# Attention stage of a hybrid layer: group norms shared out to ScalarE and GpSimd, the queries' turn at another place in the pair, the score maximum accumulated

## The chip, the cores and the metric

One core of one Trainium2 chip runs the kernel. The metric is the time of one execution on the device in microseconds, and the median of several runs counts. The core has five engines with a queue each, which they work off in order: TensorE (PE in the profile, PEld for its weight loads), VectorE (DVE), ScalarE (ACT), GpSimd (POOL) and SyncE (SP, which issues the transfers here).

## The reference, cut to what matters

One layer over 1024 latent tokens and 256 context tokens, width 1024, in float32. Half of the width goes through a convolution module, half through attention with 8 query heads on 2 key heads of 64 elements. Only the attention's part matters here:

```
u = rms_norm(x, norm_w) * (1.0 + scale) + shift
p = u @ w_in
q, k, v = qk_heads(p, q_norm_w, k_norm_w)      # each head of q and k divided by its root mean square, times a weight
q = rope_2d(q, angles)                         # x1*cos - x2*sin, x1*sin + x2*cos, by row and by column of the grid
k = rope_2d(k, angles)
k_all, v_all = concat([k_ctx, k]), concat([v_ctx, v])          # 1280 keys
s = einsum('bqkgd,bskd->bkgqs', q, k_all) / sqrt(64)
pr = softmax(s, axis=-1)
attn = einsum('bkgqs,bskd->bqkgd', pr, v_all) * silu(p[..., ZA_LO:ZA_HI])
out = concat([attn, conv]) @ w_out
h = x + gate * out
```

## The kernel before, in words

Products that need more precision than one pass gives are made from a high and a low part: "hi" is a copy rounded by the engine that writes it, "lo" the difference that is left. The kernel has four stages: the modulation and the turned tokens (`start`), the projections with the convolution taps (`project`), the attention, and the rest of the convolution module with the output projection.

The queries are made in two halves c (heads 0 to 3 and 4 to 7) and four groups g of 256 tokens. `norm_rope` (L540) takes the projected 128x512 block of a half and group from PSUM. ACT squares it, DVE sums the squares per head, DVE scales the sum and POOL raises it to the power -1/2 (`rstd`, L118). DVE multiplies the block by a cosine and by a sine table (L561, tiles q11t and the like), POOL adds the crossed halves (L567) and multiplies by the root (L568, tile q11o). `q_split` (L597) makes hi on ACT and lo on DVE, tile hl. `q_turn` (L602) turns half of a block, two heads, with four transposes on PE into a PSUM bank (qt), and ACT copies that to qT. All groups of half 0 and group 0 of half 1 are done in `project`. Groups 1 to 3 of half 1 are projected, normed, split and turned by hooks within the attention.

The attention works on pairs of heads: a unit u is one group and one head, a pair is two units, and there are 16 pairs. Within a pair each of two units has two blocks of 128 queries. For every unit and block t the steps are qa and qb (scores against 1280 keys, the part in banks of its own and the part in the shared bank of the score tile s), ma and mb (the negative maximum of each part, DVE), mc (the smaller of the two), ex (exponential on ACT with its sum, which needs the final maximum). Then for five parts k of the keys tr (four transposes of the exponentials into a PSUM bank pt), ra (raw copy out of the bank by ACT, for three of the five), hi (ACT or DVE), lo (DVE where hi is ACT's, else POOL), pv (the product with v). After that come the sum's reciprocal rz, the gate gs on POOL, ol and ad (the sum of the high and low halves), and once a pair gt, mu, mh, ml. A step is named by its kind, unit and number: lo14 is the lo part of unit 1, part 4.

What sets the order is the table ORDER: a planned time in the pair for each step, with a period of 13.4 (PERIOD) between pairs. Steps and hooks are issued in the order of these times, on each engine's queue, and the engines keep that order. The hooks have planned times of their own: QP for the two projections of a group, QN for its norm, QS for its split, QT for the turn within each of the first 14 pairs. A tile of a pool may be used again once its last reader has been issued; the engine that writes it next then waits for that reader. PSUM has two banks of tag t in this stage, which tr, gt, the turn and the projection of group 2 share. Groups 1 and 3 are projected into the bank of tag acc, which pv uses too.

The score tile s is laid out so that both blocks share one bank for 256 keys each: the part qb of one block can be written only when the exponential of the other has read the bank. This is why qb waits for an ex.

In pairs 8 to 15 another hook splits a piece of the later weights on DVE (wo0h, wo0l and so on). Behind the attention the order is left to a scheduler.

Of the kernel before, what the change touches and what calls it, by code (L numbers as in the profile page):

```python
# [11 lines left out]
BF16 = mybir.dt.bfloat16  # L12
AF = mybir.ActivationFunctionType
ALU = mybir.AluOpType
AX = mybir.AxisListType
# [3 lines left out]
P = 128  # L19
# [4 lines left out]
DH = 64  # L24
KEYS = S + CTX
# [5 lines left out]


ORDER = {
# [17 lines left out]
QP = (-2.0, -1.99), (3.9, 3.91), (7.09, 7.19)  # L51
QN = 1.32, 7.57, 8.5
QS = 6.0, 11.0, 13.45
QT = 4.0

TAP, AHEAD = 1.33, 3.0
NPT = 0, 5, 5, 5
# [23 lines left out]
class Layer:  # L81
# [455 lines left out]
        self.mc[g] = hi, lo  # L537


    def norm_rope(self, ps, nh, g, table, name):  # L540

        nc = self.nc
        n = 2 * nh
        w = n * DH
        pv = ps.rearrange("p t (h d) -> p t h d", d=DH)
        sq = self.w2([P, 2, nh, DH], f"{name}sq")
        nc.scalar.activation(sq, pv, AF.Square)
        ss = self.small([P, 16], "qss", "qss")[:, 0:n]
        nc.vector.tensor_reduce(out=ss, in_=sq.rearrange("p t h d -> p (t h) d"), axis=AX.X, op=ALU.add)
        r = self.small([P, 16], "qr", "qr")[:, 0:n]  # L550
        self.rstd(r, ss, 1.0 / DH)
        out = self.w2([P, n, DH], f"{name}o")
        if table is None:
            for t in range(2):
                nc.vector.tensor_mul(out=out[:, t * nh:(t + 1) * nh], in0=pv[:, t],
                                     in1=self.wkn.unsqueeze(1).broadcast_to([P, nh, DH]))
        else:
            t1 = self.w2([P, 2, nh, DH], f"{name}t1")
            t2 = self.w2([P, 2, nh, DH], f"{name}t2")
            for i, t in enumerate((t1, t2)):  # L560
                nc.vector.tensor_mul(out=t, in0=pv, in1=table[:, i, 2 * g:2 * g + 2, :].unsqueeze(2)  # L561
                                     .broadcast_to([P, 2, nh, DH]))
            ov, v1, v2 = (x.rearrange(s, s=2, e=16) for x, s in (
                (out, "p h (x s e) -> p s (h x) e"), (t1, "p t h (x s e) -> p s (t h x) e"),
                (t2, "p t h (x s e) -> p s (t h x) e")))
            for s in range(2):
                nc.gpsimd.tensor_add(out=ov[:, s], in0=v1[:, s], in1=v2[:, 1 - s])  # L567
        nc.gpsimd.tensor_mul(out=out, in0=out, in1=r.unsqueeze(2).broadcast_to([P, n, DH]))  # L568
        return out
# [22 lines left out]

    def q(self, c, g, ps):

        return self.norm_rope(ps, 4, g, self.tq, f"q{c}{g}")

    def q_split(self, c, g, x):  # L597
        hl = self.b4([P, 8, 2, DH], f"hl{c}{g}", F32R)
        self.split(hl[:, :, 0], hl[:, :, 1], x)
        return hl  # L600

    def q_turn(self, c, g, hl, hp):  # L602
# [47 lines left out]

    def op_ma(self, u, t):
        st = self.st[u]
        st["nm", t] = nm = self.small([P, 3], "nm", "nm")
        r = self.nc.vector.reduce_max(out=nm[:, 0:1], in_=self.s5[:, 1536 * t:1536 * t + 1024], axis=AX.X, negate=True)  # L654
        self.s_deps("DVE", r, [st["q", t, 0]])

    def op_mb(self, u, t):
        st = self.st[u]
        r = self.nc.vector.reduce_max(out=st["nm", t][:, 1:2], in_=self.s5[:, 1024 + 256 * t:1280 + 256 * t],  # L659
                                      axis=AX.X, negate=True)  # L660
        self.s_deps("DVE", r, [st["q", t, 1]])

    def op_mc(self, u, t):
        nm = self.st[u]["nm", t]
        self.nc.vector.tensor_tensor(out=nm[:, 2:3], in0=nm[:, 0:1], in1=nm[:, 1:2], op=ALU.min)  # L665

    def op_ex(self, u, t):
        nc, st = self.nc, self.st[u]
        if "z" not in st:
            st["z"] = self.small([P, 2], "z", "z")  # L670
        st["e", t] = e = self.e5.tile([P, KEYS], F32, tag="e", name=f"e{u[0]}{u[1]}{t}")
        ex = nc.scalar.activation(e, self.s5[:, t * KEYS:(t + 1) * KEYS], AF.Exp, bias=st["nm", t][:, 2:3],  # L672
                                  accum_out=st["z"][:, t:t + 1])
        self.s_deps("ACT", ex, [st["q", t, 0], st["q", t, 1]])
        self.s_use[t] = ex.ins

    def op_tr(self, u, k):
# [392 lines left out]
```

## Time and profile before

| What | Value |
|---|---|
| Median of 3 runs | 684.87 us (683.95 to 687.38) |
| The profiled execution | 683.55 us, span 681.7 us |
| PE busy | 650.2 us (95%) |
| DVE busy | 537.4 us (79%) |
| ACT busy | 352.9 us (52%) |
| POOL busy | 332.5 us (49%) |

The span is what the engines' records cover; the execution's own time lies 1.85 us above it. The attention goes from the first scores at 298.5 us to about 550 us. A share of busy time over the whole span mixes stages with different limits, so the rows are read by stage. Rows of the timeline give start, length, engine, line, operation and tiles of instructions that follow each other, how many there are, and in brackets the idle time in front and the instruction that ended it.

### The profile page before, as it was taken

How to read it: one execution, taken by the hardware profiler on the slowest of the kernel's cores; microseconds unless marked ns; L12 is line 12 of the kernel's file. 1: busy time of each engine (PE TensorE's matmuls, PEld its weight loads, DVE VectorE, ACT ScalarE, POOL GpSimd, SP SyncE). 2: the span in 40 equal slices, each digit the busy share in tenths (PEclk: the TensorE clock that was granted, in tenths of full speed). 3: DMA queues.
4: the chain of work that ended last, by engine and by line, in shares of the span. 5: the costliest groups of instructions: out<-in, count | busy, mean ns of one | idle time of the engine just before them, and what ended most of it. 6: DMA issues, size and time to landing. Idle time of an engine off the chain costs nothing.

```text
span 681.7 us, 11003 instructions
## 1 busy us (share of the span) xinstructions
PE 650.2 (95%) x4258; PEld 572.3 (84%) x4258; DVE 537.4 (79%) x844; ACT 352.9 (52%) x578; POOL 332.5 (49%) x289
## 2 busy tenths in 40 slices
PE   4989999999999999997999999899999999999997
PEld 1467799888888999996899999888888878888885
DVE  2698789749999999876999999999999953545422
ACT  3564325554343122226888888788888845441000
POOL 1244804957329132885656766565566564121200
PEclk9899999999999999999999999999999999999999
DMA  8984310312653232100010001000100021133711
GB/s 266 319 225 129 116 36 1 94 31 62 217 185 124 71 101 78 32 1 1 1 32 1 1 32 60 3 32 25 40 1 1 1 93 32 62 124 132 256 60 46
DMA packets 51251, 53.28 MB, mean 78 GB/s; under 512 B 4521, under 2 KB 41697, under 8 KB 51200
## 3 DMA queue, kind: packets, MB, share of 16 engines
q1 hardware_dynamic: 51104, 52.57, 24.4%
q8 instruction: 33, 0.54, 0.3%
q14 instruction: 18, 0.15, 0.1%
q10 hardware_dynamic: 96, 0.02, 0.0%
HBM read 44.20 MB, written 8.39 MB: 77 GB/s over the span
## 4 chain that ended last, share of the span: by engine, by line
PE 67%; DVE 23%; issue 3%; DMA 3%; ACT 2%; SPq 1%; POOL 0%; DVEq 0%; ACTq 0%
PE o L820 12%; PE pv L715 8%; PE s L636 8%; PE pt L682 7%; DVE y L456 6%; PE g L386 6%; PE a L386 6%; PE kv L412 4%; DVE yp L456 4%; PE pw L531 3%; PE zc L386 3%; PE q L412 3%; DVE p L700 3%; DVE nm L654 2%; DMA wm<-in_w_mod 2%
## 5 line engine op out<-in xcount | busy, mean ns | idle before, releaser
L706 POOL TENSOR_TENSOR p<-raw,p 128x512 fp32r<-128x512 f32 x96 | 127.0, 1337 | 81.2 <-DVE p L700 70.8
L636 PE MATMUL s<-kT,qT 128*128 128x512 f32 (+1 forms) x384 | 100.8, 372 | 4.6 <-ACT e L672 4.5
L715 PE MATMUL pv<-p,v 128*128 128x256 f32 x640 | 103.2, 292 | 0.7 <-DVE mm L747 0.7
L456 DVE SCALAR_TENSOR_TENSOR yp<-up,cw,yp 128x1024 f32<-128x1024 f32 x77 | 99.1, 1287 | 1.9
L682 PE MATMUL pt<-ident,e 128*128 128x128 f32 x640 | 93.5, 273 | 1.0 <-DVE p L706 0.8
L672 ACT ACTIVATE e<-s,nm 128x1280 f32<-128x1280 f32 x64 | 85.0, 1329 | 14.3 <-DVE nm L665 14.1
L715 PEld LDWEIGHTS pv<-p,v 128*128 128x128 f32 x640 | 85.9, 189 | 4.5 <-DVE mm L747 1.5
L654 DVE TENSOR_REDUCE nm<-s 128x1 f32<-128x1024 f32 x64 | 77.7, 1214 | 0.6
L682 PEld LDWEIGHTS pt<-ident,e 128*128 128x128 f32 x640 | 73.3, 141 | 2.6 <-PE pv L715 1.2
L636 PEld LDWEIGHTS s<-kT,qT 128*128 128x128 f32 x384 | 62.7, 189 | 11.6 <-ACT e L672 5.7
L691 ACT ACTIVATE raw<-pt 128x512 f32<-128x512 f32 x96 | 57.5, 600 | 9.6 <-PE pt L682 5.5
L700 DVE CAST p<-raw 128x512 fp32r<-128x512 f32 x96 | 47.3, 520 | 1.8 <-ACT raw L691 1.2
L698 ACT ACTIVATE p<-pt 128x512 fp32r<-128x512 f32 x64 | 38.5, 602 | 11.6 <-PE pt L682 10.3
L706 DVE TENSOR_TENSOR p<-pt,p 128x512 fp32r<-128x512 f32 x64 | 40.9, 676 | 1.4 <-ACT p L698 1.4
L456 DVE SCALAR_TENSOR_TENSOR y<-up,cw,y 128x1024 f32<-128x1024 f32 x25 | 40.8, 1632 | 0.8
L833 DVE TENSOR_TENSOR r<-o,gb 128x512 f32<-128x512 f32 (+1 forms) x17 | 10.8, 656 | 30.6 <-PE o L820 30.6
L659 DVE TENSOR_REDUCE nm<-s 128x1 f32<-128x256 f32 x64 | 26.9, 421 | 9.1 <-PE s L636 7.7
L441 POOL TENSOR_TENSOR yz<-yz,ct 128x512 f32<-128x512 f32 x24 | 33.6, 1433 | 0.0
L123 POOL TENSOR_TENSOR qr<-qr,mhalf 128x8 f32<-128x8 f32 (+1 forms) x13 | 21.5, 1657 | 9.0 <-DVE qr L122 8.8
L440 ACT ACTIVATE ct<-up,cw 128x512 f32<-128x512 f32 x24 | 15.7, 713 | 12.9 <-DVE up L424 9.9
L116 POOL TENSOR_TENSOR ul<-u,uh 128x512 fp32r<-128x512 f32 x8 | 12.2, 1528 | 20.2 <-DVE uh L114 13.6
L665 DVE TENSOR_TENSOR nm<-nm 128x1 f32<-128x1 f32 x64 | 20.2, 315 | 1.7
(578 smaller groups left out, 1751.7 us busy)
## 6 DMA issues: line engine op xcount, KB each, us to landing
x<-in_x SPq DMA_DIRECT2D x8, 512.0 KB, 5.5
wg<-in_w_mod SPq DMA_DIRECT2D x8, 512.0 KB, 4.0
xr<-in_x SPq DMA_DIRECT2D x8, 512.0 KB, 8.7
out<-r SPq DMA_DIRECT2D x15, 256.0 KB, 2.0
wm<-in_w_mod SPq DMA_DIRECT2D x12, 256.0 KB, 6.7
zc_d<-zc SPq DMA_DIRECT2D x4, 512.0 KB, 3.3
za_d<-za SPq DMA_DIRECT2D x4, 512.0 KB, 4.1
zar<-za_d SPq DMA_DIRECT2D x4, 512.0 KB
```

Source lines behind the costliest of these rows:

```text
L386: nc.tensor.matmul(acc[h], lhsT=ww, rhs=uu[k][:, h * 512:(h + 1) * 512], start=first and i == 0, stop=last and i == 2)
L412: self.nc.tensor.matmul(acc[:, t * 256:(t + 1) * 256], lhsT=x, rhs=y, start=k == 0 and i == 0, stop=k == NK - 1 and i == 2)
L456: nc.vector.scalar_tensor_tensor(out=out, in0=up[:, w:w + S], scalar=cw[:, w:w + 1], in1=y if w else st["y2"], op0=ALU.mult, op1=ALU.add)
L636: mm = nc.tensor.matmul(self.s5[:, s0 + k0:s0 + k0 + n], lhsT=qt[:, h % 4, t * P:(t + 1) * P], rhs=kT[:, w, k0:k0 + n], start=w == 0, stop ...
L654: r = self.nc.vector.reduce_max(out=nm[:, 0:1], in_=self.s5[:, 1536 * t:1536 * t + 1024], axis=AX.X, negate=True)
L672: ex = nc.scalar.activation(e, self.s5[:, t * KEYS:(t + 1) * KEYS], AF.Exp, bias=st["nm", t][:, 2:3], accum_out=st["z"][:, t:t + 1])
L682: nc.tensor.transpose(out=tp[:, i * 256 + t * P:i * 256 + (t + 1) * P], in_=st["e", t][:, (2 * k + i) * P:(2 * k + i + 1) * P], identity=s ...
L691: self.nc.scalar.activation(raw, st["T", k], AF.Copy)
L700: nc.vector.tensor_copy(out=st["p", k][:, 0], in_=st["T", k])
L706: eng.tensor_sub(out=p[:, 1], in0=st["T", k], in1=p[:, 0].bitcast(F32))
L715: nc.tensor.matmul(st["pv"][:, 0:256], lhsT=self.v[:, kt, u[1] // 4].rearrange("p w d -> p (w d)"), rhs=st["p", k][:, j, i * 256:(i + 1) * ...
L820: self.nc.tensor.matmul(o, lhsT=p, rhs=q, start=half == k == i == 0, stop=half == 1 and k == 3 and i == 2)
```

## The change

It does three things.

- The norm of groups 1 to 3 of half 1 gets a copy of the projected block from PSUM to SBUF by ACT (tile q11c and the like), the two products with the tables go from DVE to POOL, and so does the lo part of the split.
- The planned time of the queries' turn goes from 4.0 to 7.4.
- The maximum of the second part of the scores becomes one operation that multiplies by -1, takes the smaller with the first part's result as a per-row scalar, and accumulates the minimum; the separate step mc is gone, and ex reads the accumulated value. A junk tile takes the elementwise output.

```
-    "qa00": 0.0, "qb00": 1.04, "ma00": 2.04, "mb00": 2.2, "mc00": 2.74, "ex00": 3.76, "qa01": 3.85, "qb01": 4.53,
+    "qa00": 0.0, "qb00": 1.04, "ma00": 2.04, "mb00": 2.2, "ex00": 3.76, "qa01": 3.85, "qb01": 4.53,
...
 QP = (-2.0, -1.99), (3.9, 3.91), (7.09, 7.19)
 QN = 1.32, 7.57, 8.5
 QS = 6.0, 11.0, 13.45
-QT = 4.0
+QT = 7.4
...
-    def norm_rope(self, ps, nh, g, table, name):
+    def norm_rope(self, ps, nh, g, table, name, pool=False):
...
         out = self.w2([P, n, DH], f"{name}o")
+        eng = nc.vector
+        if pool:
+            eng, pc = nc.gpsimd, self.w2([P, 2, nh, DH], f"{name}c")
+            nc.scalar.activation(pc, pv, AF.Copy)
+            pv = pc
...
             for i, t in enumerate((t1, t2)):
-                nc.vector.tensor_mul(out=t, in0=pv, in1=table[:, i, 2 * g:2 * g + 2, :].unsqueeze(2)
+                eng.tensor_mul(out=t, in0=pv, in1=table[:, i, 2 * g:2 * g + 2, :].unsqueeze(2)
                                      .broadcast_to([P, 2, nh, DH]))
...
-        return self.norm_rope(ps, 4, g, self.tq, f"q{c}{g}")
+        return self.norm_rope(ps, 4, g, self.tq, f"q{c}{g}", pool=c == 1 and g > 0)
...
-        self.split(hl[:, :, 0], hl[:, :, 1], x)
+        self.split(hl[:, :, 0], hl[:, :, 1], x, lo_on="pool" if c == 1 and g else "dve")
...
     def op_mb(self, u, t):
         st = self.st[u]
-        r = self.nc.vector.reduce_max(out=st["nm", t][:, 1:2], in_=self.s5[:, 1024 + 256 * t:1280 + 256 * t],
-                                      axis=AX.X, negate=True)
+        nm = st["nm", t]
+        junk = self.sm.tile([P, 256], BF16, tag="mj", name="mj", bufs=2)
+        r = self.nc.vector.tensor_scalar(out=junk, in0=self.s5[:, 1024 + 256 * t:1280 + 256 * t], scalar1=-1.0,
+                                         scalar2=nm[:, 0:1], op0=ALU.mult, op1=ALU.min, accum_out=nm[:, 1:2])
         self.s_deps("DVE", r, [st["q", t, 1]])
-
-    def op_mc(self, u, t):
-        nm = self.st[u]["nm", t]
-        self.nc.vector.tensor_tensor(out=nm[:, 2:3], in0=nm[:, 0:1], in1=nm[:, 1:2], op=ALU.min)
+        st["mb", t] = r.ins
...
-        ex = nc.scalar.activation(e, self.s5[:, t * KEYS:(t + 1) * KEYS], AF.Exp, bias=st["nm", t][:, 2:3],
+        ex = nc.scalar.activation(e, self.s5[:, t * KEYS:(t + 1) * KEYS], AF.Exp, bias=st["nm", t][:, 1:2],
                                   accum_out=st["z"][:, t:t + 1])
-        self.s_deps("ACT", ex, [st["q", t, 0], st["q", t, 1]])
+        self.s_deps("ACT", ex, [st["q", t, 0], st["q", t, 1], st["mb", t]])
```

On ACT's queue in pair 0, this stood before (qT is the copy of the first turn, e the exponentials ex01, ex10 and ex11, hl the hi parts of groups 1 to 3; what an instruction waits for is in brackets):

```order
L112 ACTIVATE hl_3049<-q11o 128x8x64 [waits Pool_49]
L672 ACTIVATE e_3052,z<-s_2897,nm 128x1280 [waits DVE_49,PE_49]
L547 ACTIVATE q12sq<-q_2983 128x512 [waits Activation_49]
L547 ACTIVATE q13sq<-q_3054 128x512 [waits PE_49]
L698 ACTIVATE p_3142<-pt_3137 128x512 [waits PE_49]
L112 ACTIVATE hl_3155<-q12o 128x8x64 [waits Pool_49]
L672 ACTIVATE e_3160,z<-s_2897,nm 128x1280 [waits DVE_49]
L691 ACTIVATE raw_3163<-pt_3150 128x512 [waits PE_49,Activation_49]
L691 ACTIVATE raw_3176<-pt_3170 128x512 [waits PE_49]
L112 ACTIVATE hl_3188<-q13o 128x8x64 [waits Pool_49]
L672 ACTIVATE e_3191,z<-s_2897,nm 128x1280 [waits DVE_49]
```

And this stands there now:

```order
L676 ACTIVATE e_3047,z<-s_2897,nm 128x1280 [waits DVE_49]
L617 ACTIVATE qT_3098<-qt_3099 128x512 [waits PE_49]
L547 ACTIVATE q12sq<-q_2985 128x512
L556 ACTIVATE q12c<-q_2985 128x512
L547 ACTIVATE q13sq<-q_3049 128x512 [waits Activation_49]
L556 ACTIVATE q13c<-q_3049 128x512
L702 ACTIVATE p_3148<-pt_3143 128x512 [waits PE_49]
L112 ACTIVATE hl_3161<-q12o 128x8x64 [waits Pool_49]
L676 ACTIVATE e_3166,z<-s_2897,nm 128x1280 [waits DVE_49]
L695 ACTIVATE raw_3169<-pt_3156 128x512 [waits PE_49,Activation_49]
L112 ACTIVATE hl_3194<-q13o 128x8x64 [waits Pool_49]
```

Before, the first turn's copy stood ahead of the hi part of group 1; now it stands behind ex01 and ahead of the square of group 2, and the two hi parts still stand directly ahead of ex10 and of ex11 (which follows the last row).

On POOL's queue in the same pair, before (power, the two sums and the last product of group 2, then the power of group 3):

```order
L123 TENSOR_TENSOR qr<-qr,mhalf 128x8 [waits DVE_49]
L567 TENSOR_TENSOR q12o<-q12t_3111,q12t_3112 128x16x16 [waits DVE_49,Activation_49]
L567 TENSOR_TENSOR q12o<-q12t_3111,q12t_3112 128x16x16
L568 TENSOR_TENSOR q12o<-q12o,qr 128x512 [waits Pool_49]
L123 TENSOR_TENSOR qr<-qr,mhalf 128x8 [waits DVE_49]
```

And now:

```order
L123 TENSOR_TENSOR qr<-qr,mhalf 128x8 [waits DVE_49]
L566 TENSOR_TENSOR q12t_3115<-q12c,tq 128x512 [waits Activation_49]
L566 TENSOR_TENSOR q12t_3116<-q12c,tq 128x512
L572 TENSOR_TENSOR q12o<-q12t_3115,q12t_3116 128x16x16 [waits Pool_49]
L572 TENSOR_TENSOR q12o<-q12t_3115,q12t_3116 128x16x16
L573 TENSOR_TENSOR q12o<-q12o,qr 128x512 [waits Pool_49]
```

The two products with the table stand between the power and the sums of each group; before, the sums followed the power at once.

On PE's queue in a later pair, around the turn, before (tr11, the shared scores qb01 and tr12 stand behind it):

```order
L636 MATMUL s_2897<-kT_74,qT_3427 128x512 x4
L609 MATMUL qt_3855<-identr,hl_3049 128x128 [waits DVE_49,PE_49]
L609 MATMUL qt_3855<-identr,hl_3049 128x128 x3
L715 MATMUL pv_3796<-p_3721,v 128x256 x4
L682 MATMUL pt_3865<-ident,e_3753 128x128 [waits DVE_49]
```

And at its new place (tr14 ahead of it, the shared scores qb10 and tr00 behind it):

```order
L686 MATMUL pt_3919<-ident,e_3759 128x128 [waits DVE_49]
L686 MATMUL pt_3919<-ident,e_3800 128x128
L686 MATMUL pt_3919<-ident,e_3759 128x128
L686 MATMUL pt_3919<-ident,e_3800 128x128
L614 MATMUL qt_3929<-identr,hl_3044 128x128 [waits Activation_49]
L614 MATMUL qt_3929<-identr,hl_3044 128x128 x3
L641 MATMUL s_2897<-kT_74,qT_3501 128x256 x2
L686 MATMUL pt_3943<-ident,e_3848 128x128 [waits Activation_49]
```

The turn now waits for ACT instead of DVE, and two score matmuls stand between it and the transpose that waits for ACT.

## Rows read from the trace of the kernel before

**Rows 1.** Busy time by stretch, a pair each: us, PE, PEld, DVE, ACT, POOL, PEclk, DMA, GB/s.

```profile
298.50:320.86 22.36, 18.68 (x143) 17.54 (x141) 16.23 (x27) 10.63 (x17) 14.42 (x14) 1.00 0.00 1
...
364.12:378.48 14.36, 14.36 (x114) 13.54 (x111) 13.35 (x29) 12.71 (x23) 9.45 (x9) 1.00 0.01 2
...
437.05:452.50 15.45, 14.56 (x113) 13.47 (x112) 14.96 (x31) 12.68 (x23) 9.28 (x9) 1.00 0.00 0
...
514.30:529.30 15.00, 14.53 (x109) 13.34 (x108) 14.82 (x30) 12.25 (x22) 9.26 (x9) 1.00 0.00 1
529.30:544.00 14.70, 14.20 (x107) 13.02 (x106) 14.55 (x28) 11.99 (x21) 9.27 (x9) 1.00 0.01 2
```

**Rows 2.** PE's groups, pairs 8 to 13: count, busy us, mean ns, idle and releaser.

```profile
L609 PE MATMUL qt<-identr,hl 128*128 128x128 f32 x24 | 3.1, 251 | 5.3 <-DVE p L706 5.3
```

**Rows 3.** The same view of DVE, 422 to 530 us.

```profile
L665 DVE TENSOR_TENSOR nm<-nm 128x1 f32<-128x1 f32 x28 | 7.4, 264 | 0.7
```

**Rows 4.** Timeline of DVE in pair 9: mb10 and mc10.

```profile
448.44 0.42 DVE L659 TENSOR_REDUCE nm<-s 128x1 f32<-128x256 f32 x1
448.90 0.56 DVE L665 TENSOR_TENSOR nm<-nm 128x1 f32<-128x1 f32 x1
```

**Rows 5.** Timeline of POOL at the same time.

```profile
448.70 0.74 POOL L768 TENSOR_TENSOR mal<-ma,mah 128x256 fp32r<-128x256 f32 x1
```

**Rows 6.** Timeline of PE in pair 4: the turn, pv14, then qb10 and tr00.

```profile
369.06 0.46 PE L609 MATMUL qt<-identr,hl 128*128 128x128 f32 x4
369.35 0.71 PE L715 MATMUL pv<-p,v 128*128 128x256 f32 x4
...
373.89 0.49 PE L636 MATMUL s<-kT,qT 128*128 128x256 f32 x2
374.21 0.60 PE L682 MATMUL pt<-ident,e 128*128 128x128 f32 x4
```

**Rows 7.** Timeline of ACT: the copy of that turn.

```profile
369.55 0.60 ACT L612 ACTIVATE qT<-qt 128x512 fp32r<-128x512 f32 x1 [0.21 <-PE qt L609]
```

**Rows 8.** Timeline of ACT in pair 0: square of group 2, ex10, ex11.

```profile
310.33 0.59 ACT L547 ACTIVATE q12sq<-q 128x512 f32<-128x512 f32 x1
...
318.25 1.33 ACT L672 ACTIVATE e<-s,nm 128x1280 f32<-128x1280 f32 x1 [1.48 <-DVE nm L665]
...
321.79 1.31 ACT L672 ACTIVATE e<-s,nm 128x1280 f32<-128x1280 f32 x1
```

**Rows 9.** Timeline of PE in pairs 0 and 1: turn, scores, projection of group 3, waits.

```profile
306.35 0.46 PE L609 MATMUL qt<-identr,hl 128*128 128x128 f32 x4
307.75 1.44 PE L636 MATMUL s<-kT,qT 128*128 128x256 f32 x6 [0.95 <-ACT e L672]
309.03 0.28 PE L412 MATMUL q<-wq10h,uh 128*128 128x256 f32 x1
...
314.78 0.40 PE L636 MATMUL s<-kT,qT 128*128 128x256 f32 x2
...
319.72 0.50 PE L636 MATMUL s<-kT,qT 128*128 128x256 f32 x2 [2.73 <-ACT e L672]
...
323.25 0.50 PE L636 MATMUL s<-kT,qT 128*128 128x256 f32 x2 [0.78 <-ACT e L672]
...
326.43 0.51 PE L609 MATMUL qt<-identr,hl 128*128 128x128 f32 x4 [1.10 <-DVE p L706]
```

**Rows 10.** Timeline of POOL in pair 0: power and last product of group 2.

```profile
311.92 1.65 POOL L123 TENSOR_TENSOR qr<-qr,mhalf 128x8 f32<-128x8 f32 x1 [7.03 <-DVE qr L122]
...
315.04 1.04 POOL L568 TENSOR_TENSOR q12o<-q12o,qr 128x512 f32<-128x512 f32 x1
```

**Rows 11.** Line 206, POOL's product that makes a table: ns least, median, most.

```profile
L206 POOL TENSOR_TENSOR tq<-cs,wq x1: 2387/2387/2387, 77.6 to 77.6; 128x1024 f32<-128x1024 f32 x1
```

**Rows 12.** The view of rows 1 for a stretch of the first stage, and pair 0.

```profile
16.00:18.00 2.00, 2.00 (x6) 0.59 (x5) 1.43 (x3) 0.00 (x0) 0.00 (x0) 0.50 1.22 305
...
316.00:320.00 4.00, 1.27 (x9) 0.90 (x8) 3.93 (x9) 2.52 (x5) 3.51 (x4) 1.00 0.01 2
```

More of the change, by code (lines that the diff above doesn't have):

```diff
@@ L652, in op_ma @@
         st = self.st[u]
-        st["nm", t] = nm = self.small([P, 3], "nm", "nm")
+        st["nm", t] = nm = self.small([P, 2], "nm", "nm")
         r = self.nc.vector.reduce_max(out=nm[:, 0:1], in_=self.s5[:, 1536 * t:1536 * t + 1024], axis=AX.X, negate=True)
```

6 rows, old and new, of the table ORDER are left out of this document.

## Prediction, before the run

> **What bounds the kernel now.** I read the time of each pair first, then who ends the idle time of TensorE (PE) in each kind of pair, then the rows around the two places where the change moves work. Sixteen pairs of heads (counted 0 to 15 here) make the attention stage. Cut at the first own-key scores of each pair, they fall into three kinds [rows 1]. Pair 0 takes 22.36 us, with PE busy for 18.68: the stage is being filled, and the last three query groups are projected in it. Pairs 2 to 7 (one row stands for the six) take 14.36 us each and PE is busy for all 14.36, while VectorE (DVE) works 13.35: here PE is the bound, and a faster DVE is worth nothing. Pairs 8 to 13 (again one row) take 15.45 us with PE at 14.56 and DVE at 14.96; pair 14 takes 15.00 and pair 15 14.70. They also carry the split of the output weights on DVE. The idle time of PE in pairs 8 to 13 stands before the queries' turn, 5.3 us over the six turns and put down to DVE's lo part [rows 2]: here DVE is the bound. So DVE work taken away can pay in pairs 8 to 15 alone, down to PE's floor. That floor is 14.36 in a pair with a turn, and 14.36 less the turn's 0.29 in pairs 14 and 15, which have none: at most 6 x 1.09 + 0.93 + 0.63 = 8.1 us.
>
> **The accumulated maximum.** Per pair it removes four one-column minima (mc), mean 264 ns in pairs 8 to 14 [rows 3], about 1.06 us of DVE. It changes four 256-element reductions (mb) into a tensor_scalar with an accumulated output. The nearest row is the reduction itself, 0.42 us from the same bank [rows 4]. No row of DVE shows an accumulated output. From below, the new mb costs what the old one did; from above, the accumulator adds a step like the mc that it replaces, and nothing is saved. Mb now waits for ma, as mc waited for mb: I take that as even. The longest minima are long for a reason: the mc at 448.90 lasts 0.56 and ends at 449.46, two hundredths after the GpSimd instruction that began at 448.70 and lasted 0.74 [rows 4, 5]. The new mb reads PSUM and one scalar, so I take that wait to go rather than to move. The Trainium skill's SBUF — State Buffer, section "SBUF: two separate sides", says that GpSimd and a DVE operation with two SBUF inputs take one port pair in turn, each for a whole instruction; the trace agrees at that place, and by the rule mb would not inherit the wait. I take 0.6 us of DVE per pair, between 0 and 1.06: 15.45 becomes 14.85. Pairs 2 to 7 get nothing from it.
>
> **The turn in the middle of the pair.** The queries' turn leaves its place after the own-key scores and stands between the last transpose of one head and the shared scores of the next. Its wait for DVE's lo part goes with it, but what follows it is new. Only two banks of tag t exist. At the old place three more pieces of PE work stood between the turn and the next user of its bank. At the new place two short score matmuls stand there, and then the first transpose of the next head takes the bank that ScalarE (ACT) has just copied the turn out of: the other bank's last reader, lo14, is not issued yet. In a PE-bound pair the turn starts at 369.06, the copy at 369.55 and it lasts 0.60 [rows 6, 7]: from the turn's start to a free bank 1.09 us, some 0.06 more for the signal. PE has 0.29 of turn (369.06 to 369.35) and 0.32 of scores (373.89 to 374.21) to do meanwhile [rows 6]. It stands still for 1.15 - 0.61 = 0.54 us, in every pair with a turn, and everything behind that transpose on PE's queue stands with it. Lower bound 0 (the transpose finds another bank), upper 0.9 if ACT comes late, since the copy now also delays mh, hi14 and hi00 behind it. I take 0.54: PE's floor becomes 14.90. Pairs 2 to 7: 6 x 0.54 = +3.2 us. Pairs 8 to 13: DVE at 14.85 and PE at 14.90, with a tenth for two engines so nearly level, 15.0: 6 x -0.45 = -2.7 us. Pairs 14 and 15 have no turn and keep DVE as the bound: 2 x -0.45 = -0.9 us.
>
> **The norms on GpSimd, and the start.** For groups 1 to 3 DVE loses two products and a lo part each, about 6 us in all, in pair 0 and ahead of it. GpSimd (POOL) gains them, ACT a copy. The price is in the order. ACT's queue has the hi part of group 2 in front of ex10, and that of group 3 in front of ex11. Each waits for POOL's last product. Before, these came in time: ex10 ran at 318.25, ex11 at 321.79 [rows 8]. Two things make them late.
> First, ACT's copy of the first turn now stands ahead of the square of group 2 on ACT's queue, and on PE the turn stands behind the 48 matmuls that project group 3. Before, the square ran at 310.33 [rows 8]. Now PE goes from 306.35 straight to the 1.28 us of scores (307.75 to 309.03; the wait of 0.95 before them is gone, since ex00 no longer stands behind DVE's products) and to the projection (309.03 to 314.78 before, thus 307.63 to 313.38) [rows 9]. Turn 0.46, copy 0.60: the square runs from 314.4 to 315.0, 4 us later than before. From the square's end at 310.92 to the power on POOL at 311.92 is 1.00 us of DVE's sum and scaling [rows 8, 10]; now 315.95.
> Second, POOL's chain of a group was 4.16 us (power at 311.92 to the end of the last product, 316.08 [rows 10]). It gets two products of 512 elements in front of the sums. The nearest rows are a product with a broadcast operand over 1024 elements, 2.39 us, so 1.20 for half [rows 11], and one of 512 elements, 1.04 [rows 10]. I take 1.2, bounds 1.04 and 1.5. A group takes 4.16 + 2.4 = 6.56 us, and groups 2 and 3 follow each other: the products end at 322.5 and 329.1. A hi part of 0.6 behind each: ex10 starts at 323.1 instead of 318.25, ex11 at 329.7 instead of 321.79 [rows 8]. The shared scores that waited for ex10 at 319.72 and for ex11 at 323.25 [rows 9] come 4.9 and 7.9 us later, and PE has nothing else in its queue that it may do.
> Of the 7.9 us, 1.10 come back where PE waited for DVE at 326.43 [rows 9], and 0.51 as the turn moves on; 0.8 of that goes again on the turn at its new place and its bank, and about a microsecond waiting for pair 1's first exponential, which stands right behind the late start. Start: 7.9 - 1.6 + 0.8 + 1.0 = +8.1 us (bounds 6.5 with quick products and no second wait, 10 with slow ones).
> PE then stands still for 8 us with one short burst. Its granted clock was 0.50, the lower level of 1.2 GHz, at 16 to 18 us after a mostly idle stretch, and 1.00, the upper, at 316 to 320 with a wait of 2.73 us [rows 9, 12]. A lower clock after the long wait costs between 0 and 3 us; much of what PE does first is followed by waits anyway, so I take 1.
> Tail: the scheduler puts some of the transposes and output products behind the attention in another order, with the same work; 0, between -1 and +1.
>
> **Sum.** 8.1 + 1.0 + 3.2 - 2.7 - 0.9 = +8.7 us. The profiled run took 683.55 (span 681.7), so 692.3; the median of the runs is 684.87, 1.3 above it. Against the median: 693.6 us.
>
> **Rivals.**
> A, faster: the start is not held. If POOL's chain stayed hidden, because ex10 and ex11 did not wait for it, PE would gain its waits of 0.95, 2.73 and 1.10 [rows 9] at the start, say 4 us, and pairs 8 to 15 could gain the 2.7 + 0.9 to 8.1 above, with 3.2 lost in pairs 2 to 7: 684.87 - 4.4 to 684.87 - 8.9, about 678. It decides if the products on POOL end before 318.2 and 321.2; by the row of the projection's end plus 6.56 us a group they cannot. 6 in 100.
> B, no change: the start as forecast, but no stall behind the turn, and DVE's relief takes pairs 8 to 15 to PE's floor: +8.1 - 8.1 = 684.9. It needs another free bank at the transpose, or a copy within 0.6 us of the turn's start; the row gives 1.09. 12 in 100, with mixtures that end inside 681.4 to 688.3.
> C, slower still: the accumulated output takes a second step on DVE, and pairs 8 to 15 stay at 15.45, 15.00 and 14.70: 693.6 + 3.6 = 697.2. The Trainium skill's VectorE: DVE Perf Modes, section "Two Vector instructions with no wait between them", says that a DVE operation which writes out an accumulator is two instructions, and by that this rival's mechanism would be there; how long the second lasts no run here shows. 14 in 100.
> D, slower still: the clock falls for the whole refill, +2 more, and POOL's products run at 1.5: 693.6 + 2 + 1.9 = 697.5. 13 in 100.
> My forecast: 55 in 100.
>
> **Range and chances.** A and the lower half of B lie outside, and the far end of C with D together (701): 685.5 to 700. A difference under 0.5% (3.4 us) is about what a measurement of this kernel can't tell from no change. Faster: 0.06, from A. Same: 0.12, B. Slower: 0.82.
>
> **What would show it.** In the trace after: ex10 and ex11 of pair 0 at about 323 and 330, each right behind a hi part that waited for POOL; PE's shared scores waiting for ACT's exponential twice, 13 us or so together; pair 0 near 27 us. In pairs 2 to 7, a wait of some 0.5 us before the transpose behind the turn, put down to ACT's qT, and pairs of 14.9 us; pairs 8 to 13 near 15.0. No qt waiting for DVE. Mb at 0.42 us and no mc. I am wrong if pairs 2 to 7 stay at 14.36 (the bank), if pairs 8 to 13 fall to 14.4 (then DVE was worth more), or if ex11 starts before 325 (then POOL's chain is shorter than I worked out, or something went ahead of it).

## The result, and the profile after

The changed kernel takes 705.33 us (median of 4 runs, 705.08 to 706.35). The kernel before took 684.41 us beside it, so the ratio is 1.030 (95% interval 1.027 to 1.033): slower by 21 us, where 9 had been forecast. The profiled execution has a span of 703.1 us against 681.7, +21.4.

Busy time by pair, the view of [rows 1] cut at the same marks, of the kernel after: pairs 0, 4, 9 and 14.

```profile
298.31:326.53 28.22, 19.68 (x142) 18.50 (x141) 11.97 (x21) 12.29 (x20) 20.28 (x19) 0.88 0.00 1
374.96:389.92 14.96, 14.58 (x114) 13.63 (x112) 12.56 (x28) 12.41 (x23) 9.44 (x9) 1.00 0.00 1
450.88:466.89 16.01, 15.13 (x114) 13.66 (x112) 14.56 (x30) 12.58 (x23) 9.35 (x9) 1.00 0.00 0
530.90:545.98 15.08, 14.59 (x109) 13.29 (x108) 14.29 (x29) 12.15 (x22) 9.29 (x9) 1.00 0.00 1
```

Pair 0 went from 22.36 to 28.22 us, pair 4 from 14.36 to 14.96, pair 14 from 14.94 to 15.08 (pair 15's first own-key scores stood at 529.20, so the row of 15.00 in [rows 1] ends 0.1 late). Pair 9 is the surprise: DVE's busy time did fall, 14.96 to 14.56, and the pair still grew from 15.45 to 16.01.

ACT in pair 0 of the kernel after (timeline; it answers [rows 8]):

```profile
313.56 0.60 ACT L617 ACTIVATE qT<-qt 128x512 fp32r<-128x512 f32 x1 [4.60 <-PE qt L614]
314.05 0.59 ACT L547 ACTIVATE q12sq<-q 128x512 f32<-128x512 f32 x1
...
322.39 0.63 ACT L112 ACTIVATE hl<-q12o 128x512 fp32r<-128x512 f32 x1 [5.79 <-POOL q12o L573]
322.93 1.31 ACT L676 ACTIVATE e<-s,nm 128x1280 f32<-128x1280 f32 x1
...
329.34 0.63 ACT L112 ACTIVATE hl<-q13o 128x512 fp32r<-128x512 f32 x1 [2.67 <-POOL q13o L573]
329.87 1.31 ACT L676 ACTIVATE e<-s,nm 128x1280 f32<-128x1280 f32 x1
```

The square of group 2 runs at 314.05 (forecast 314.4), ex10 at 322.93 (323.1) and ex11 at 329.87 (329.7), each right behind a hi part that waited for POOL. PE's rows of the same time show what waited for them:

```profile
324.38 0.80 PE L641 MATMUL s<-kT,qT 128*128 128x256 f32 x2 [8.15 <-ACT e L676]
...
331.32 0.80 PE L641 MATMUL s<-kT,qT 128*128 128x256 f32 x2 [1.88 <-ACT e L676]
```

Busy time and granted clock (the third number from the end) of three stretches, the first of them within the wait of 8.15 us:

```profile
320.00:324.00 4.00, 0.00 (x0) 0.00 (x0) 0.68 (x1) 1.61 (x2) 3.92 (x5) 0.50 0.00 0
324.00:328.00 4.00, 3.62 (x14) 3.33 (x15) 2.38 (x4) 1.41 (x4) 3.92 (x4) 0.50 0.00 0
332.00:336.00 4.00, 4.00 (x17) 3.51 (x16) 3.08 (x6) 2.52 (x5) 2.58 (x3) 0.50 0.00 0
```

The clock fell within the wait of 8.15 us, PE worked on at 1.2 GHz behind it, and it stayed there until about 337 us.

PE around the turn in pair 4 (it answers [rows 6]):

```profile
384.38 0.55 PE L614 MATMUL qt<-identr,hl 128*128 128x128 f32 x4
384.76 0.47 PE L641 MATMUL s<-kT,qT 128*128 128x256 f32 x2
385.61 0.66 PE L686 MATMUL pt<-ident,e 128*128 128x128 f32 x4 [0.38 <-ACT qT L617]
```

This is the forecast stall for the bank, and it stands behind every turn. Shown as idle it is 0.38; with the rows around it, which last longer than undisturbed ones (0.66 against 0.60), the pair pays 0.6.

To see where the 21.4 us lie, the span is cut at five marks: the first scores, the first exponential of pairs 2, 8 and 14, and the last exponential (us; the forecast's terms stand beside them).

| Stage | before | after | difference | forecast |
|---|---|---|---|---|
| up to the first scores | 298.50 | 298.31 | -0.2 | 0 |
| start, to pair 2 | 40.70 | 50.51 | +9.8 | 8.1 + 1.0 |
| pairs 2 to 7 | 87.60 | 91.27 | +3.7 | +3.2 |
| pairs 8 to 13 | 92.68 | 96.04 | +3.4 | -2.7 |
| pairs 14, 15, to the last exponential | 25.05 | 25.65 | +0.6 | -0.9 |
| tail | 137.17 | 141.32 | +4.2 | 0 |

A stage cut at exponentials can hold a piece of the next kind of pair: the 87.60 us are five intervals of 14.36 and one of 15.80, since the first exponential of pair 8 already waits for the longer work there. Two stages came as forecast. Three did not, and those three make 11.8 of the 12.7 us that the forecast missed in the profiled run.

### The profile page after: what moved, and what is told of

It reads as the page before. It is cut to its first block, busy times and chain, and to the rows that moved or that the text cites. A ratio compares the mean times of both kernels' runs of the same rounds, so it can differ in the third digit from the quotient of the medians.

```text
span 703.1 us, 11055 instructions
## 1 busy us (share of the span) xinstructions
PE 660.3 (94%) x4258; PEld 579.1 (82%) x4258; DVE 523.1 (74%) x835; ACT 351.4 (50%) x581; POOL 343.6 (49%) x298
## 4 chain that ended last, share of the span: by engine, by line
PE 69%; DVE 19%; ACT 3%; DMA 3%; issue 3%; POOL 2%; SPq 1%; DVEq 0%; ACTq 0%; POOLq 0%
PE o L824 12%; PE pt L686 9%; PE s L641 9%; PE pv L719 8%; DVE y L456 6%; PE g L386 6%; PE a L386 6%; PE kv L412 4%; DVE yp L456 4%; PE q L412 4%; PE pw L531 3%; PE zc L386 3%; DVE p L704 2%; DMA wm<-in_w_mod 2%; PE mrow L264 2%
## 5 line engine op out<-in xcount | busy, mean ns | idle before, releaser
L641 PE MATMUL s<-kT,qT 128*128 128x512 f32 (+1 forms) x384 | 103.4, 379 | 10.1 <-ACT e L676 10.0
L686 PE MATMUL pt<-ident,e 128*128 128x128 f32 x640 | 97.2, 280 | 9.9 <-ACT qT L617 5.3
L686 PEld LDWEIGHTS pt<-ident,e 128*128 128x128 f32 x640 | 74.8, 144 | 15.6 <-ACT qT L617 8.2
L641 PEld LDWEIGHTS s<-kT,qT 128*128 128x128 f32 x384 | 64.7, 194 | 18.7 <-ACT e L676 12.6
L666 DVE TENSOR_SCALAR_CACHE_REDUCE mj<-s,nm 128x256 bf16<-128x256 f32 x64 | 30.9, 483 | 24.9 <-PE s L641 21.3
L440 ACT ACTIVATE ct<-up,cw 128x512 f32<-128x512 f32 x24 | 15.7, 714 | 12.9 <-DVE up L424 9.9
L625 ACT ACTIVATE za<-za 128x512 f32<-128x512 f32 x8 | 4.8, 597 | 29.3 <-PE za L412 29.3
```

Of the source, the lines that this page charges most:

```text
L641: mm = nc.tensor.matmul(self.s5[:, s0 + k0:s0 + k0 + n], lhsT=qt[:, h % 4, t * P:(t + 1) * P], rhs=kT[:, w, k0:k0 + n], start=w == 0, stop ...
L686: nc.tensor.transpose(out=tp[:, i * 256 + t * P:i * 256 + (t + 1) * P], in_=st["e", t][:, (2 * k + i) * P:(2 * k + i + 1) * P], identity=s ...
```

## The experiments

The theory after the result had three parts. In pairs 8 to 13 the chain of waits that sets the pair's length goes round one loop, a stretch of DVE and then a stretch of PE, so that what either does on its own stretch adds, and what it does beside the other's stretch doesn't. At the start, the turn's place holds ACT, and through it POOL's chain. The tail's loss belongs to no part of the change. The table has every run by the same stages, as differences (to about 0.1 us) of its one profiled run to that of before; the last column is the ratio of the medians of all runs with its interval.

| Kernel | first scores | start | 2 to 7 | 8 to 13 | 14, 15 | tail | ratio |
|---|---|---|---|---|---|---|---|
| after | -0.2 | +9.8 | +3.7 | +3.4 | +0.6 | +4.2 | 1.030 (1.027 to 1.033) |
| turn alone | +2.3 | +5.4 | +3.4 | +2.5 | 0.0 | +4.3 | 1.022 (1.019 to 1.025) |
| maximum alone | 0.0 | -1.9 | 0.0 | +0.5 | +0.4 | +2.6 | 1.001 (0.999 to 1.003) |
| norms alone | +0.6 | +3.5 | 0.0 | -0.1 | +0.1 | +2.6 | 1.009 (1.007 to 1.012) |
| after, turn back | +1.1 | +2.4 | +0.1 | +0.4 | +0.6 | +2.5 | 1.010 (1.006 to 1.014) |
| after, first turn back | +0.1 | +3.9 | +3.7 | +3.4 | +0.6 | +4.2 | 1.022 (1.020 to 1.024) |
| before, turn twice | +1.2 | +0.9 | +2.0 | +2.1 | +0.1 | +2.6 | 1.010 (1.008 to 1.013) |
| before, turn at 10.3 | +0.1 | +1.6 | +6.5 | +7.1 | 0.0 | +2.8 | 1.028 (1.025 to 1.032) |
| maximum, turn at 3.9 | +0.2 | +2.5 | 0.0 | +0.5 | +0.4 | +2.5 | 1.008 (1.005 to 1.011) |
| before without mu | +0.2 | 0.0 | 0.0 | 0.0 | 0.0 | -0.3 | 1.000 (0.998 to 1.002) |
| before, split on POOL | +1.9 | +0.6 | -1.1 | -3.6 | -0.8 | +2.7 | 0.996 (0.995 to 0.998) |
| maximum and split on POOL | +1.1 | -1.5 | -1.4 | -3.9 | -0.4 | +1.4 | 0.988 (0.985 to 0.991) |

The first column varies by 2.5 us from kernel to kernel though the engines' instructions ahead of the first scores are the same in all: single profiled runs differ by that much there. The two that are latest, turn alone and split on POOL, had a mean granted clock of 0.97 from 50 to 100 us, the kernel before 1.00.

**The turn alone.** The kernel before with

```
-QT = 4.0
+QT = 7.4
```

> The kernel before with the turn's planned time at 7.4 and nothing else. Theory (PE and DVE stand in one loop in pairs 8 to 13, so the turn's wait for its bank adds there too): pairs 2 to 7 take 14.95 us, pairs 8 to 13 take 16.0 instead of 15.45; in pair 0 the square of group 2 runs at 314, ex10 at about 320.4 and ex11 at 324.6 (321.79 before), so the start costs 2.8. Together 2.8 + 3.6 + 3.3 = +9.7 us, about 694. Rival (the slower of two engines sets the pair): pairs 8 to 13 stay at 15.45 since DVE's work is the same, together +6.4, about 691.

Measured: 700.11 us (ratio 1.022), with pairs of 14.93 and 15.86, where the theory had 14.95 and 16.0. The rival, with 15.45 in pairs 8 to 13, is out: they pay for the turn although DVE has no more work. The median was missed by 6 us and the profiled run by 8: 4.3 in the tail, 2.3 ahead of the first scores, a start of 5.4 instead of 2.8, and 1.0 less than expected in the pairs. The square of group 2 ran 17.3 us after the first scores, against 15.7 in the changed kernel: without the relief that the other two parts give DVE in pair 0, the scores ahead of the projection come later too (ex00 runs 7.8 us after the first scores, against 4.0), and the turn behind it with them.

**The maximum alone.** The kernel before with the new op_mb, without mc, and nothing else of the diff.

> The kernel before with the accumulated maximum and nothing else. Theory: only the minima that stand in the loop's DVE part are saved, and the new mb is longer by a like amount: pairs 8 to 13 at 15.3 to 15.45, pairs 2 to 7 at 14.36, total within 1.5 us of before (about 683.5). Rival (the slower of two engines sets the pair): DVE's busy time falls by 0.4 us a pair and pairs 8 to 15 with it, 8 x -0.4 = -3.2, about 681.

Measured: 686.10 us, ratio 1.001 with an interval that holds 1. Pairs 8 to 13 take 15.52, not less than before, which puts the rival out (15.05 a pair by it). The start gains 1.9, the tail loses 2.6. DVE's groups of the kernel after in pairs 8 to 13 show what became of the minima of [rows 3] and the reduction of [rows 4]:

```profile
L666 DVE TENSOR_SCALAR_CACHE_REDUCE mj<-s,nm 128x256 bf16<-128x256 f32 x24 | 11.6, 484 | 4.6 <-PE s L641 2.4
...
L666 DVE DVE_READ_ACCUMULATOR mj<-s,nm 128x1 f32 x24 | 2.0, 83 | 0.0
```

The operation is two instructions, 484 and 83 ns. So the mechanism of rival C is there; together they are 0.15 us over the old reduction's 0.42 and 0.11 under reduction and minimum together (0.42 + 0.26). The wait beside a POOL instruction that had made single minima long (0.56 in [rows 4]) did go, as forecast: all 64 of the new operation in the kernel after take 472 to 486 ns.

**The norms alone.** The kernel before with the norm_rope and q_split part of the diff.

> The kernel before with the norms of three groups shared out to ACT and POOL, and nothing else. Theory: the square of group 2 stays at 310.3, POOL's chain of a group takes 6.7 us instead of 4.2, ex10 at about 319.2 and ex11 at about 325.8 (321.79 before): start +4.0, of which the 1.1 us wait at pair 1's turn comes back; pairs 2 to 13 as before. About +3, 688. Rival (the chain on POOL is what costs the whole start of the change, whatever the turn does): +8 or more, 693.

Measured: 691.16 us. The pairs stay, the start costs 3.5 (3 expected), and the tail costs 2.6, which had not been expected. POOL's products in this kernel (timeline of pair 0), two a row:

```profile
313.10 2.54 POOL L566 TENSOR_TENSOR q12t<-q12c,tq 128x512 f32<-128x512 f32 x2
...
319.83 2.50 POOL L566 TENSOR_TENSOR q13t<-q13c,tq 128x512 f32<-128x512 f32 x2
```

One takes 1.25 to 1.27 us (forecast 1.2). The norms alone are far from the whole start, so the rival is out.

**After, with the turn back.** The changed kernel with `QT = 4.0`.

> The changed kernel with the turn's planned time back at 4.0 (norms shared out, accumulated maximum kept). Theory: start as in the kernel with the norms alone, about +3; pairs 2 to 7 at 14.36, pairs 8 to 13 at 15.3 to 15.45; about 687. Rival (the slower of two engines sets the pair): pairs 8 to 15 lose 0.4 each, about 684.5. Second rival (the tail's 4 us hang on the new maximum's order, not on the turn): about 691.

Measured: 691.65 us, 13.7 below the changed kernel: two thirds of the loss hang on the turn. The total lies at the second rival's 691. The start (+2.4) is the theory's; pairs 8 to 13 (15.52) lie a little above its 15.3 to 15.45 and do not fall by the first rival's 0.4; the tail (+2.5) is what the theory had left out. The second rival's cause doesn't hold: the norms alone, without the new maximum, have the same tail.

**After, with the first turn alone back.**

```
-                        add((2 * i + hp) * PERIOD + QT, ...
+                        add((2 * i + hp) * PERIOD + (QT if i + hp else 4.0), ...
```

> The changed kernel with the first turn alone (the one in pair 0) back at 4.0, the other thirteen at 7.4. Theory (in pair 0 the copy of the first turn stands ahead of the square of group 2 on ACT, and the turn behind the projection of group 3 on PE, so POOL's chain starts 4 us late): ex10 back to about 319.2, ex11 to 326.1, start 6 us less late than in the changed kernel; pairs 2 to 7 still 14.95, pairs 8 to 13 still 16.0. About 699. Rival (the late start is POOL's products alone, and the first turn's place costs nothing): no change, 705.

Measured: 699.72 us, as expected. ACT in pair 0 of this kernel:

```profile
306.96 0.60 ACT L617 ACTIVATE qT<-qt 128x512 fp32r<-128x512 f32 x1 [2.91 <-PE qt L614]
...
309.28 0.60 ACT L547 ACTIVATE q12sq<-q 128x512 f32<-128x512 f32 x1
...
325.19 1.31 ACT L676 ACTIVATE e<-s,nm 128x1280 f32<-128x1280 f32 x1
```

With the copy at 306.96 the square runs 4.8 us earlier than in the changed kernel, and ex11 4.7 earlier. One turn of fourteen is worth 5.9 us of the start (9.8 against 3.9), and no other stage moved by more than 0.3.

**Before, each turn but the first two made twice.** One line of the edit is shown; `again` is 2 for all turns but the two of pairs 0 and 1 (the text below, written ahead of the run, says "but the first").

```
-        for i in range(2):
+        for i in [0, 1] * again:
```

> The kernel before, in which each turn but the first makes its four transposes twice into the same bank (0.29 us of PE more; no other engine gets work). Theory (PE and DVE stand in one loop, so PE's part adds although DVE has no less work): pairs 2 to 7 14.65 and pairs 8 to 13 15.74, both +0.29. Rival (the slower engine sets the pair, DVE in pairs 8 to 13, and PE has 0.9 us idle there): pairs 2 to 7 14.65, pairs 8 to 13 stay at 15.45. The tail has the order of the other experiments, +2.5: about 691 by the theory, 689 by the rival.

Measured: 691.63 us; pairs 2 to 7 14.70, pairs 8 to 13 15.81. Both grew by 0.34 to 0.37, though in pairs 8 to 13 PE waits 0.88 us a pair for DVE. PE's waits in pairs 9 to 13 of this kernel are, to the last digit, those of the kernel before:

```profile
PE qt L609 <- DVE p L706: 4.4, 5, 0.9
```

The row gives the sum, how many and the longest. Work on PE is not hidden by that wait: the wait comes later by as much. The rival is out.

**Before, without the product with the gate.** DVE has 0.42 us less a pair, in the stretch where PE works.

```
-        st["m"] = self.w2([P, 256], f"ma{u[0]}{u[1]}")
-        self.nc.vector.tensor_mul(out=st["m"], in0=st["gt"][:, 0:256], in1=st["mm"])
+        st["m"] = st["mm"]
```

> The kernel before without the product with the gate (mu, 0.42 us of DVE a pair): that part of the computation is left out, and the unmultiplied sum goes on. In the trace it lies where PE works and DVE keeps up with it. Theory (loop): pairs 8 to 13 stay at 15.45, or lose 0.1; about 0 in the pairs, +2.5 if the tail has the other order: 685 to 687. Rival (the engine with the most work sets the pair): DVE's busy time falls from 14.96 to 14.54 and pairs 8 to 15 fall by 0.4 each, -3.2: about 682 to 684.

Measured: 684.45 us, ratio 1.000. The total lies between the theory's 685 and the rival's 684, so the pairs decide. Five pairs from the first exponential of pair 9 on, of the kernel before and of this one:

```profile
442.27:519.48 77.21, 72.90 (x553) 67.84 (x554) 74.86 (x147) 63.42 (x111) 46.45 (x45) 1.00 0.07 22
```

```profile
442.42:519.67 77.25, 72.95 (x553) 67.86 (x554) 71.81 (x142) 62.78 (x110) 46.25 (x45) 1.00 0.07 22
```

DVE's busy time fell from 74.86 to 71.81, 0.6 us a pair (the minima got shorter as well), and the five pairs are the same to 0.04 us. A busy share of 97% was not the bound, and the rival is out.

**Before, with the split's lo part on POOL.** DVE has some 0.6 us less a pair, in the stretch where PE waits.

```
-                    self.split(hi, lo, x, hi_on="dve")
+                    self.split(hi, lo, x, hi_on="dve", lo_on="pool")
```

> The kernel before, in which the lo part of the weights' split (0.61 us of DVE a pair, at the start of pairs 8 to 15) goes to POOL. Theory (PE and DVE stand in one loop; this operation lies in the stretch where DVE works and PE waits): pairs 8 to 13 fall by about 0.6, 15.45 to 14.85, pairs 14 and 15 too; -4.8 in the pairs, +2.5 by the tail's other order, about 682.5. Rival (POOL takes the port that DVE's copies behind the split need, and they stand still as long): pairs 8 to 13 at 15.45 or above, about 687.

Measured: 682.50 us, ratio 0.996. Pairs 9 to 13 take 14.94. DVE work, which was worth nothing in the experiment before, is worth 0.5 a pair here. Five pairs from the first exponential of pair 9 on, then two rows in pair 9, DVE and POOL:

```profile
442.60:517.32 74.72, 73.47 (x552) 68.47 (x553) 70.10 (x142) 63.84 (x110) 55.02 (x51) 1.00 0.07 22
```

```profile
454.02 1.08 DVE L700 CAST p<-raw 128x512 fp32r<-128x512 f32 x3
...
454.23 2.01 POOL L116 TENSOR_TENSOR wo1l<-wo01s,wo1h 128x512 fp32r<-128x512 f32 x1 [1.39 <-PE pt L682]
```

The rival had the wrong loser: the three copies behind the split take 1.08 us here, and 2.10 in the kernel before (chain below), where one of them stood 1.51 us beside a lo part of POOL. Here POOL's lo part takes 2.01 instead of some 1.3. The Trainium skill's SBUF — State Buffer, section "SBUF: two separate sides", says that a GpSimd operation and a DVE operation in a two-port mode or with two SBUF inputs share a port pair, which the one that starts first holds for its whole length. By that rule each of the two would wait as the rows show it.

So the edit did more than was meant. DVE's stretch lost the lo part's 0.69 and 1.02 of the copies, some 1.7 us, and DVE's busy time 0.95 a pair; the pair got only 0.5 shorter. The chain of this kernel shows why: in pair 9 it stays on PE but for one piece of POOL.

```profile
456.21 1.27 POOL p L706
```

PE's waits for DVE are gone (4.4 us over the five pairs before), and waits for POOL of 1.6 us stand there instead. The forecast of 0.6 came nearly true, but not because the pair follows DVE's stretch one to one: it does so only until another chain is longer.

**Before, with the turn at 10.3.** `QT = 10.3`, between the next head's first transpose and its scores.

> The kernel before with the turn at 10.3: between the next head's first transpose and its own-key scores, so four matmuls of 512 columns and four of 256 stand behind the turn before the next transposes. Theory (what 7.4 costs a pair is the copy out of the bank, less the PE work that stands between the turn and the bank's next user): no wait for qT, pairs 2 to 7 at 14.36, pairs 8 to 13 at 15.45 or a little less; in pair 0 the square of group 2 is ahead of the first turn's copy, so ex11 stays at 321.8. With the tail's other order (+2.5) about 687. Rival (any place behind the last transpose of the old head costs the same): pairs 2 to 7 at 14.95, pairs 8 to 13 at 15.85, about 694.

Measured: 703.32 us; both the theory's 687 and the rival's 694 missed. Pairs 2 to 7 take 15.44, pairs 8 to 13 16.63. The wait for qT is gone, as expected, but this stands there instead:

```profile
379.69 0.51 PE L609 MATMUL qt<-identr,hl 128*128 128x128 f32 x4 [0.89 <-DVE p L706]
```

The turn takes the bank whose last reader is lo14 on DVE, and that comes late at this place. The theory had looked at what stands behind the turn and not at who frees the bank ahead of it.

**The maximum alone, with the turn at 3.9.**

> The kernel with the accumulated maximum alone, with the turn at 3.9 instead of 4.0. That moves the first turn ahead of the projection of group 2 on PE in pair 0, and the order of the tail is then that of the kernel before. Theory (the tail's 2.5 us are the scheduler's other order, and hang on no part of the change): start and pairs as with the accumulated maximum alone, last exponential at about 543.5, tail as before; about 683.7. Rival (the tail's 2.5 us belong to the new maximum): 686.

Measured: 690.25 us. The premise was false: the tail of the kernel that ran has the other order, so this says nothing on the tail. And the start, taken as unmoved, cost 4.4 us more than with the maximum alone: the first turn, now ahead of the projection of group 2, waits 2.61 us for the lo part that DVE makes of its input, and that projection and the shared scores wait behind it on PE, where before the projection had run in the meantime.

**The maximum, and the split's lo part on POOL.**

> The kernel with the accumulated maximum alone and the lo part of the weights' split on POOL. The tail's order differs from that of the kernel before in two places only. Theory: start as with the accumulated maximum alone (-1.9), pairs 8 to 13 at 15.53 - 0.6 = 14.9 (-3.2), pairs 14 and 15 -0.8, tail 0: about 679. Rival (the accumulated maximum lengthens the DVE stretch by what the split saves): 15.45 a pair, about 683.

Measured: 677.02 us, ratio 0.988 (0.985 to 0.991). This is faster than both kernels. Pairs 9 to 13 take 14.87. The pairs gained 5.7 us where 4.0 had been expected; the tail, taken as 0, cost 1.4 in the profiled run, which at 678.75 is the slowest of the four.

**The tail over all runs.** Behind the last scores, the changed kernel, and nine of the eleven experiments, have one and the same order of PE's instructions, whatever their edit; without mu and the last kernel stay near that of before. Tails in the other order last 139.7 to 140.0 us in seven kernels, and 141.3 to 141.5 in three (after, turn alone, first turn back). What those three have in their profiled runs is a lower clock in one stretch. The stretch and the one ahead of it, first of the kernel after, then of the one with the maximum alone:

```profile
576.78:581.78 5.00, 2.75 (x18) 1.85 (x16) 2.17 (x4) 1.92 (x4) 3.01 (x3) 1.00 0.15 58
581.78:586.78 5.00, 4.93 (x28) 4.73 (x29) 3.29 (x9) 3.52 (x6) 0.11 (x1) 0.66 0.01 3
```

```profile
558.55:563.55 5.00, 2.76 (x18) 1.86 (x16) 2.17 (x4) 1.93 (x4) 3.00 (x3) 1.00 0.14 51
563.55:568.55 5.00, 4.93 (x35) 4.47 (x36) 3.31 (x10) 4.38 (x8) 0.91 (x1) 1.00 0.00 0
```

The kernel with maximum and split has PE's order of before but for two instructions and the lower clock (0.66 too): 138.6, 1.4 over before. So the tail's 4.2 us are some 2.5 that go with the order and 1.6 with the clock. Why the same instructions after the same pause are clocked down in the profiled runs of four kernels and not in the others stays open. It need not be the kernel: the runs of one kernel differ in the same way. Maximum and split took 678.75 (the profiled run) and 678.50 us with a mean granted clock of 0.991 over the span, and 675.52 and 675.53 with 0.996. Only one run of each kernel has a trace, so where the clock was lower in the others is not shown.

## Why the prediction was wrong in size

**The sign and the start: right, in part by luck.** The square, ex10 and ex11 came within half a microsecond, by the mechanism named: the first turn's copy ahead of the square (5.9 us, the kernel with the first turn back), POOL's products at 1.25 (1.2 taken) ahead of ex10 and ex11. Pair 0 was longer than named, 28.22 us against 27, and PE's two waits for the exponentials shorter, 8.15 + 1.88 = 10.0 against 13, since PE worked at the lower clock between them. The term of "about a microsecond waiting for pair 1's first exponential" did not come: behind 331.32 PE shows no wait before the next turn's bank. The lower clock stands in its place. PE's eight pieces of scores and transposes from 331.32 to 338.12 take 6.80 us; the same four pieces in a row take 2.10 in the kernel before (327.35 to 329.45), so twice that, 4.20, and by this estimate the lower clock cost up to 2.6, against the 1 taken. No run measured it by itself. The parts are not additive at the start: turn, maximum and norms alone give 5.4 - 1.9 + 3.5 = 7.0 of the 9.8. What makes the rest was not isolated; before, ex10 waited 1.48 us for DVE [rows 8], and a delay of one part alone can hide there.

**The turn in pairs 2 to 7: right.** 0.54 a pair forecast, 0.57 in the turn's own kernel and 0.6 in the changed one.

**Pairs 8 to 13: the step that failed**, 6.1 of the 12.7 us. The prediction took the pair as the larger of two loads, and DVE's relief as a gain of 0.45 a pair: "DVE at 14.85 and PE at 14.90, with a tenth for two engines so nearly level, 15.0". DVE's busy time did fall, by 0.40 of the 0.6 us taken, but the pairs got 0.56 longer. The chain of waits in the kernel before shows why the larger load doesn't give the pair (pair 9; start, length):

```profile
437.00 0.42 DVE mm L747
...
437.78 0.69 DVE wo0l L116
438.48 2.10 DVE p L700 x3
440.57 1.13 DVE nm L654
...
442.31 0.60 DVE p L706
...
443.04 0.51 PE qt L609 x4
...
451.63 0.25 PE s L636 x2
...
451.91 0.44 DVE nm L659
```

From 437.00 to 442.9 only DVE is on the chain, from 443.04 to 451.9 only PE, and then DVE again: one loop of 6.6 + 8.9 us. Each engine is busy during the other's stretch too, which makes DVE's 97%, but with work that has time. The same places after:

```profile
452.22 2.10 DVE p L704 x3
454.32 1.14 DVE nm L659
...
456.20 0.60 DVE p L710
...
456.94 0.63 PE pt L686 x4
457.57 0.50 PE s L641 x2
...
461.61 0.31 PE qt L614 x4
...
461.93 0.61 ACT qT L617
...
462.59 0.66 PE pt L686 x4
...
466.30 0.49 DVE mj L666 x2
```

PE's stretch, from its first row to DVE's mb, went from 8.87 (443.04 to 451.91) to 9.36 us (456.94 to 466.30): the bank's wait is in it. DVE's, the rest of the pair, went from 6.58 to 6.65: of the four minima hardly any had stood on the chain, and mb with its accumulator read waits for ma. Sum +0.56, which is the pair. [rows 2] had been read as "here DVE is the bound"; it says only that PE waited there. Turn twice, without mu and split on POOL show it from three sides: PE's work adds, DVE's beside PE doesn't count, DVE's ahead of PE does, as long as DVE is on the chain.

**Pairs 14 and 15**: the same step, DVE taken as the bound; -0.9 forecast, +0.6 measured. The maximum alone has +0.4 there, the turn alone 0.0.

**The tail: the second step that failed**, "the same work; 0, between -1 and +1". Another order and a lower clock went with 4.2 us. The bound of 1 had no row behind it.

**The rivals.** C's mechanism is real, but what it foresaw as the upper end (pairs 8 to 15 unchanged) still left out the loop, and D's lower clock over the whole refill came, and came again in the tail. POOL's products at 1.5, the other half of D, did not; its 1.9 for them was too much as well, since two products in each of two groups at 0.3 more make 1.2. None of them, and no combination, reached 705. A and B went as the rows had said: the start was held, and no other bank was free.

## What to carry to other kernels

When two engines are both near full and each has waits that the other ends, lay the chain over one period before adding up loads: if it changes engine only once there and back, the period is a sum, and only work on the chain's stretch counts, until another chain is longer. Price a moved step at three places: behind whom its input is read, who frees its buffer ahead of it, and who wants the buffer next. And give the part behind the change that a scheduler orders a bound from its waits, not from its work, since an edit far from it can change its order.

## What the hardware showed that was not expected

- An accumulated tensor_scalar over 128x256 elements from PSUM takes 484 ns, and 83 ns more for an instruction of its own that reads the accumulator; the plain reduction took 0.42 us. The Trainium skill's VectorE: DVE Perf Modes, section "Two Vector instructions with no wait between them", says that such an operation is two instructions; the trace agrees and gives the length.
- A copy on DVE of 128x512 elements from SBUF to SBUF took 0.42 us, or 1.51 (at 439.06 in the kernel before) beside a lo part on POOL that had begun 0.1 us before it; a lo part on POOL took 2.01 (split on POOL) instead of some 1.3 where DVE's copies had begun first.
- PE's granted clock fell to 1.2 GHz within a wait of 8.15 us and stayed there for some 17 us, from 320 to 337, although PE was busy for 4.00 of 4.00 us from 332 to 336. In the tail, the same pause of 2.25 of 5 us was followed by the lower clock in the profiled runs of four kernels, and by the full one in the others. Runs of one and the same kernel differed too: 0.991 against 0.996 over the span, and 678.6 us against 675.5.
